# Up-projection of two FFNs by seven block products instead of eight

## The chip, the cores and the metric

The kernel runs on one core of a Trainium2 chip. Its engines work side by side, each on its own list of instructions in order: TensorE (PE), with its weight loads shown apart (PEld), VectorE (DVE), ScalarE (ACT), GpSimd (POOL), and SyncE (SP), which here issues all the DMAs. The metric is the time of one execution on the device in microseconds. Times before: 1180.17 us, the median of three runs (1176.22 to 1181.59).

## The reference

Two trunk layers over 512 latent tokens of 1024 channels, with 256 context tokens. Layer 0 has attention as its mixer, layer 1 a Fourier transform over channels and tokens; each layer ends in a gated FFN with a convolution of width 3 over the tokens. Around each sub-layer stand RMS norms and a modulation (shift, scale, gate) that is computed from a conditioning vector. What matters here is the FFN:

```
def conv_ffn(h, w_up, conv_w, conv_b, w_down):
    u = h @ w_up                                   # (512, 1024) @ (1024, 2 * 2816)
    up = jnp.pad(u, ((0, 0), (1, 1), (0, 0)))
    u = up[:, :-2] * conv_w[0] + up[:, 1:-1] * conv_w[1] + up[:, 2:] * conv_w[2] + conv_b
    gate, val = jnp.split(u, 2, axis=-1)
    return (jax.nn.silu(gate) * val) @ w_down      # (512, 2816) @ (2816, 1024)
...
x = x + g2 * rms_norm(conv_ffn(h, ffn_w_up[i], ...), norm_g[i, 3])
```

## The kernel before, in words

Channels lie on the 128 partitions, tokens along the free axis: `xT` is the stream, `yT` a sub-layer's result, each 8 channel tiles (`KC`) by 512 tokens in fp32. Every product is made of three: an operand is split into a high part (an ACT cast to fp32r, `h`) and a low part (DVE: source minus high part, `l`), and `mm3` (lines 89 to 92) issues high x high, high x low, low x high. `split` (L112, its two instructions on L113) does this for weights and activations. `hh` and `hl` hold the two parts of the FFN's input.

An FFN has 22 channel tiles `fi` of 128 hidden channels, each with a gate part and a value part. For one `fi`, `up_weights` (L943) loads 1 MB of weights (`raw`, three buffers, L120), splits the two halves (128 x 1024 each) into `wh` and `wl` (`wpair`, four buffers, L125), and `up_mm` (L979) makes 8 x 3 products of 512 columns for each half, into one PSUM bank (tag `mm`, six banks). `conv` (L984) turns the bank into a convolved tile `cv`: ACT does the middle tap and the bias (L994), DVE the other two taps (L995, L997), reading PSUM. `gated` (L1006) does the Silu on ACT (L1007), the product on DVE (L1008), and splits the result into a pair from `Pairs` (seven pairs of buffers of two tiles each), where it waits for the down-projection.

The first three `fi` (the six units in `first`, L1016 to L1083) are made while the input's second token half is still being worked out: in the first FFN they run beside the end of the attention's output boundary, in the second beside the end of the Fourier layer's, where the token factors and the shift are applied after the products (`fix`, L989 to L1001). `remod` and `mod_tiles` (L212, L282) make the modulated input: h = x * am * R + bm, then its two parts, odd channel tiles with POOL's help.

The rest goes by `HALVES`: 14 `fi`, then 8. After each part follows the down-projection over its `fi`, for 8 output tiles `d`: `weights(d)` loads and splits, `part(d, hs)` multiplies; the first part is copied to `yT` by ACT, the second added by DVE (L1102). In the second part the output tiles are first made for token half 0 (tile 0 for both), then `mid` starts what follows with that half, and the seven products for half 1 (L1134) are made beside it. In the first FFN, `gemv_jobs` (L368) computes the modulation of layer 1 meanwhile: 24 loads of 1 MB (`in_mod_r`), 48 operations of 1024 elements on DVE (L376, L379). It is a generator, and `pump` advances it: once after each `fi` and twice after each output tile `d` of the first part (`GP = [1, 2]`).

The order on each engine is that of a scheduler which takes the text's order and lets an instruction pass where an earlier one is not ready; `follow` and `fence` fix an order by hand. Buffers rotate in the order of allocation, so that a load for `raw` waits until the third buffer before it has been used up.

Of the kernel before, what the change touches and what calls it, by code (L numbers as in the profile page):

```python
# [10 lines left out]
F32 = mybir.dt.float32  # L11
F32R = mybir.dt.float32r
# [17 lines left out]
HALVES = [(0, 14), (14, 8)]  # L30
# [4 lines left out]
# what is traced where: how far work of one kind runs ahead of another kind's  # L35
# [32 lines left out]
def kernel(ctx: ExitStack, tc: tile.TileContext, a):  # L68
# [20 lines left out]
    def mm3(out, ah, al, bh, bl, start, stop):  # L89
        i = PE.matmul(out, lhsT=ah, rhs=bh, start=start, stop=False)  # L90
        PE.matmul(out, lhsT=ah, rhs=bl, start=False, stop=False)  # L91
        return i, PE.matmul(out, lhsT=al, rhs=bh, start=False, stop=stop)  # L92

    # issued after another one on the same engine
# [4 lines left out]
    # work that must not be issued ahead of the last instruction traced before a fence on its engine  # L99
# [61 lines left out]
    # products that keep the PE's clock up where it would have to wait  # L161
# [4 lines left out]
    # sums over channels: four column tiles of the PE hold a quarter of the tokens each  # L166
# [5 lines left out]
    # 1 / sqrt(sum / D + eps)  # L172
# [10 lines left out]
    # the same where only the time until the end counts: sums on all partitions at once  # L183
# [14 lines left out]
    # one quarter of the tokens per quadrant of partitions: side by side, then to all partitions  # L198
# [12 lines left out]
    # h = x * am * R + bm for several channel tiles, shared out over the engines  # L211
    def mod_tiles(items, R):  # L212
        for i, (h, l, src, am, bm) in enumerate(items):
            t = mk(cp, [P, HT], F32, "md_t", 4)
            if i % 2:
# [11 lines left out]
    # squares of y: summed over channel tiles by GpSimd, the last one by the PE  # L227
    class YStat:
# [8 lines left out]
        def add(self, pps, src, hs):  # L237
# [9 lines left out]
            # the halves of the last one share a tile where they come one after the other  # L247
# [26 lines left out]
    # x += gate * rms_norm(y) for one channel tile  # L274
# [7 lines left out]
    def remod(h, am, bm, R, ks=range(KC)):  # L282
        hs = halves[h]
        mod_tiles([(hh[:, k, hs], hl[:, k, hs], xT[:, k, hs], am[:, k:k + 1], bm[:, k:k + 1]) for k in ks], R)

    # x += gate * rms_norm(y); then the next sub-layer's modulated input
# [56 lines left out]
        # the factors: tokens on partitions, or on all partitions  # L343
# [23 lines left out]
    # adaLN off the critical path: products and sums on DVE, the sum over partitions on the PE  # L367
# [30 lines left out]
    # the same on the PE: four column tiles take a quarter of the columns each  # L398
# [27 lines left out]
    # output projection's weights for two channel tiles  # L426
# [10 lines left out]
    with ExitStack() as es:  # L437
# [998 lines left out]
```

## Time and profile before

| what | value |
|---|---|
| median of three runs | 1180.17 us |
| span of the profiled execution | 1176.5 us |
| its own time | the span is from the first instruction to the last; the median of the runs lies 3.7 us above it |
| PE busy | 1134.0 us, 6878 products, as many weight loads |
| DVE busy | 751.6 us, 1215 instructions |
| ACT busy | 512.2 us, 887 instructions |
| POOL busy | 201.1 us, 213 instructions |
| moved by DMA | 145.18 MB, mean 123 GB/s |

The page of the profile gives the busy time of each engine, and the span in 40 slices; further down the chain of work that ended last, and the groups of instructions that cost most, by line, engine and operation. A group's row reads: line, engine, operation, output <- inputs, shapes, count | busy us, mean ns of one | idle time of the engine just before, and what ended it. A row of a timeline reads: start in us, duration in us, engine, line, operation, output <- inputs, shape, count, and in brackets how long the engine sat idle before and what released it. Durations on DVE, ACT and PE hold an end that overlaps the next instruction, so that neighbours' starts lie closer together than the durations say. A row of the windows gives for a stretch of the span its length and the busy time of each engine in it, then the TensorE clock granted (1.00 is full speed), the busy share of the DMA engines and GB/s. `mm<-hh,wh` is an up-projection, `mm<-xh,wh` a down-projection.

### The profile page before, as it was taken

How to read it: one execution, taken by the hardware profiler on the slowest of the kernel's cores; microseconds unless marked ns; L12 is line 12 of the kernel's file. 1: busy time of each engine (PE TensorE's matmuls, PEld its weight loads, DVE VectorE, ACT ScalarE, POOL GpSimd, SP SyncE). 2: the span in 40 equal slices, each digit the busy share in tenths (PEclk: the TensorE clock that was granted, in tenths of full speed). 3: DMA queues.
4: the chain of work that ended last, by engine and by line, in shares of the span. 5: the costliest groups of instructions: out<-in, count | busy, mean ns of one | idle time of the engine just before them, and what ended most of it. 6: DMA issues, size and time to landing. Idle time of an engine off the chain costs nothing.

```text
span 1176.5 us, 17135 instructions
## 1 busy us (share of the span) xinstructions
PE 1134.0 (96%) x6878; PEld 946.1 (80%) x6878; DVE 751.6 (64%) x1215; ACT 512.2 (44%) x887; POOL 201.1 (17%) x213
## 2 busy tenths in 40 slices
PE   7999999999999999999999998988999999999995
PEld 4689898679898877777878998877788888888895
DVE  4673777675779685756665568988966532255555
ACT  3332356566554434322444445646644332234342
POOL 1132534222320000000000153663000000000013
PEclk9999999999999999999999999998999999999998
DMA  9432110874115353666622301621233222332112
GB/s 371 187 127 72 37 36 7 298 306 152 65 43 209 108 208 110 237 238 225 233 90 56 116 11 35 210 81 60 72 108 103 73 84 99 108 108 72 54 55 72
DMA packets 27127, 145.18 MB, mean 123 GB/s; under 512 B 2724, under 2 KB 7460, under 8 KB 14120
## 3 DMA queue, kind: packets, MB, share of 16 engines
q1 hardware_dynamic: 27048, 144.09, 35.0%
q8 instruction: 54, 0.88, 0.3%
q14 instruction: 25, 0.20, 0.1%
HBM read 141.98 MB, written 2.10 MB: 122 GB/s over the span
## 4 chain that ended last, share of the span: by engine, by line
PE 84%; DVE 11%; DMA 1%; ACT 1%; issue 1%; POOL 1%; SPq 0%; DVEq 0%; ACTq 0%; POOLq 0%
PE mm L90 24%; PE mm L92 23%; PE mm L91 23%; DVE md_t L278 2%; PE PT L786 2%; PE gm L405 1%; DVE hl L333 1%; PE O L90 1%; DVE wl L113 1%; DVE xT L280 1%; PE S L90 1%; PE O L91 1%; PE O L92 1%; PE S L92 1%; DMA xT<-in_xT 1%
## 5 line engine op out<-in xcount | busy, mean ns | idle before, releaser
L113 DVE TENSOR_TENSOR wl<-raw,wh 128x1024 fp32r<-128x1024 f32 (+1 forms) x139 | 167.6, 1210 | 207.8 <-ACT wh L113 207.5
L90 PE MATMUL mm<-hh,wh 128*128 128x512 f32 (+2 forms) x728 | 276.1, 379 | 0.0
L92 PE MATMUL mm<-hh,wl 128*128 128x512 f32 (+2 forms) x728 | 275.7, 379 | 0.0
L91 PE MATMUL mm<-hl,wh 128*128 128x512 f32 (+2 forms) x728 | 275.4, 378 | 0.0
L113 ACT CAST wh<-raw 128x1024 fp32r<-128x1024 f32 (+2 forms) x151 | 149.6, 999 | 183.4 <-PE mm L91 141.9
L90 PEld LDWEIGHTS mm<-hh,wh 128*128 128x128 f32 x728 | 137.7, 189 | 29.3 <-issue 1.2
L92 PEld LDWEIGHTS mm<-hh,wl 128*128 128x128 f32 x728 | 137.7, 189 | 27.9
L91 PEld LDWEIGHTS mm<-hl,wh 128*128 128x128 f32 x728 | 137.8, 189 | 27.5
L253 POOL TENSOR_TENSOR gacc<-gacc,sq 128x256 f32<-128x256 f32 (+1 forms) x35 | 31.5, 900 | 681.3 <-ACT sq L251 680.5
L90 PE MATMUL mm<-xh,wh 128*128 128x512 f32 (+1 forms) x368 | 131.5, 357 | 0.0
L91 PE MATMUL mm<-xl,wh 128*128 128x512 f32 (+1 forms) x368 | 130.6, 355 | 0.0
L92 PE MATMUL mm<-xh,wl 128*128 128x512 f32 (+1 forms) x368 | 130.5, 355 | 0.0
L90 PEld LDWEIGHTS mm<-xh,wh 128*128 128x128 f32 x368 | 69.2, 188 | 12.4 <-issue 1.2
L91 PEld LDWEIGHTS mm<-xl,wh 128*128 128x128 f32 x368 | 69.1, 188 | 11.1
L92 PEld LDWEIGHTS mm<-xh,wl 128*128 128x128 f32 x368 | 69.0, 187 | 11.0
L113 ACT CAST xh<-cv 128x512 fp32r<-128x512 f32 x44 | 27.3, 620 | 100.9 <-DVE cv L1008 100.9
L995 DVE SCALAR_TENSOR_TENSOR cv<-mm,cols,cv 128x511 f32<-128x511 f32 x83 | 61.8, 745 | 11.4 <-ACT cv L994 11.4
L994 ACT ACTIVATE cv<-mm,cols 128x512 f32<-128x512 f32 x83 | 64.2, 774 | 10.4 <-PE mm L92 10.4
L997 DVE SCALAR_TENSOR_TENSOR cv<-mm,cols,cv 128x511 f32<-128x511 f32 x83 | 62.2, 749 | 2.2
L1007 ACT ACTIVATE cv<-cv 128x512 f32<-128x512 f32 x44 | 27.8, 631 | 71.2 <-DVE cv L997 68.7
L379 DVE SCALAR_TENSOR_TENSOR gacc<-raw,scol,gacc 128x1024 f32<-128x1024 f32 x42 | 53.8, 1281 | 4.5 <-DMA raw<-in_mod_r 4.1
L91 PE MATMUL mm<-hl,xh 128*128 128x256 f32 (+1 forms) x160 | 47.3, 296 | 3.6 <-DVE hl L333 2.8
(358 smaller groups left out, 2238.7 us busy)
## 6 DMA issues: line engine op xcount, KB each, us to landing
raw<-in_w_up SPq DMA_DIRECT2D x44, 1024.0 KB, 5.0
raw<-in_mod_r SPq DMA_DIRECT2D x24, 1024.0 KB, 5.0
raw<-in_mod_p SPq DMA_DIRECT2D x16, 1024.0 KB, 6.4
raw<-in_w_down SPq DMA_DIRECT2D x16, 896.0 KB, 4.6
raw<-in_w_down SPq DMA_DIRECT2D x16, 512.0 KB, 3.7
raw<-in_w_in SPq DMA_DIRECT2D x6, 1024.0 KB, 5.0
raw<-in_w_out SPq DMA_DIRECT2D x4, 1024.0 KB, 6.0
raw<-in_w_f SPq DMA_DIRECT2D x8, 512.0 KB, 4.4
```

Of the source, the lines that this page charges most:

```text
L90: i = PE.matmul(out, lhsT=ah, rhs=bh, start=start, stop=False)
L91: PE.matmul(out, lhsT=ah, rhs=bl, start=False, stop=False)
L92: return i, PE.matmul(out, lhsT=al, rhs=bh, start=False, stop=stop)
L113: i = S.copy(out=h, in_=src), eng.tensor_tensor(out=l, in0=src, in1=f(h), op=ALU.subtract)
L253: G.tensor_tensor(out=self.acc[:, sl], in0=self.acc[:, sl], in1=sq[:, sl], op=ALU.add)
L278: m = V.scalar_tensor_tensor(out=t, in0=yT[:, k, hs], scalar=der[:, l, gi, k:k + 1], in1=R, op0=ALU.mult, op1=ALU.mult)
L379: held(V.scalar_tensor_tensor(out=acc, in0=w[:, i, :], scalar=scol[:, 0, k:k + 1], in1=acc, op0=ALU.mult, op1=ALU.add))
L786: PE.transpose(out=pt[:, j * P:(j + 1) * P], in_=Ps[j][:, off:off + P], identity=ident)
L994: S.activation(out=cv, in_=ps, func=AF.Identity, bias=bc, scale=wc[1])
L995: V.scalar_tensor_tensor(out=cv[:, 1:], in0=ps[:, :T - 1], scalar=wc[0], in1=cv[:, 1:], op0=ALU.mult, op1=ALU.add)
L997: V.scalar_tensor_tensor(out=cv[:, :T - 1], in0=ps[:, 1:], scalar=wc[2], in1=cv[:, :T - 1], op0=ALU.mult, op1=ALU.add)
L1007: S.activation(out=cg, in_=cg, func=AF.Silu)
```

## The change

For the 19 `fi` behind the first three, in both FFNs, the up-projection is made in blocks. The input is cut in two over channels (4 tiles each) and in two over tokens (256 each), the weights in two over channels and into gate and value: a 2 x 2 by 2 x 2 product, done by Strassen's scheme (in Winograd's form) with seven block products. Each is 4 x 3 products of 256 columns.

- `seven_inputs`, once for each FFN, forms four combinations of the input's blocks on DVE. It needs the unsplit input, so `remod` now leaves it in `yT` (`kept` in `mod_tiles`; even channel tiles get one more ACT instruction). It splits the four into three pairs of `spare` buffers and, for the fourth, over the place of `hh` and `hl` for channels 0 to 3 of token half 1.
- `seven_weights`, for each `fi`, forms four combinations of the weights' blocks on POOL (128 x 512 each) in a second `raw` buffer, and splits seven blocks instead of four: 3 of 128 x 512, 2 of 128 x 1024, in four `wpair` buffers.
- `seven_products` makes the products in two PSUM banks. Where banks hold sums, ACT copies a partial result out before another product is added on top; POOL adds two of them, DVE makes three sums. The result is `u` in SBUF (one buffer), and `conv` now reads it there instead of in PSUM.
- `HALVES` (14, 8) becomes `GROUPS` (8, 8, 6): three down-projections, the second and the third added to `yT`. `Pairs` shrinks from seven pairs to four, and three `spare` ones. All groups begin their first two output tiles without the last `fi`, which before was so in the last part only.
- `gemv_jobs` is no longer pumped after each `fi`, but twice after each output tile `d` of groups one and two (`GP = 2`).

```diff
-HALVES = [(0, 14), (14, 8)]
+GROUPS = [(0, 8), (8, 8), (16, 6)]
+FIRST = 3
-GP = [1, 2]
+GP = 2
...
+            if kept is not None and i % 2 == 0:
+                V.scalar_tensor_tensor(out=t, in0=src, scalar=am, in1=R, op0=ALU.mult, op1=ALU.mult)
+                S.activation(out=t, in_=t, func=AF.Identity, bias=bm, scale=1.0)
+                S.copy(out=h, in_=t)
+                V.tensor_tensor(out=l, in0=t, in1=f(h), op=ALU.subtract)
...
+    def seven_inputs(xp):
+        (b11, b12), (b21, b22) = blocks_of(yT)
+        hi, lo = blocks_of(hh), blocks_of(hl)
+        V.tensor_tensor(out=b11, in0=b12, in1=b11, op=ALU.subtract)
+        V.tensor_tensor(out=b12, in0=b22, in1=b12, op=ALU.subtract)
+        V.tensor_tensor(out=b22, in0=b22, in1=b11, op=ALU.subtract)
+        V.tensor_tensor(out=b21, in0=b21, in1=b22, op=ALU.subtract)
+        t3, t2, t4 = (xp.spare([P, KH, HT]) for _ in range(3))
+        t1 = hi[0][1], lo[0][1]
+        for (h, l), src in ((t3, b12), (t1, b11), (t2, b22), (t4, b21)):
+            split(h, l, src)
...
+    def seven_weights(l, fi):
+        r = raw([P, 2, KC, P], a["w_up"][l, fi])
+        s = mk(wp, [P, 4, KH, P], F32, "raw", 3)
+        (a11, a12), (a21, a22) = [[r[:, i, c * KH:(c + 1) * KH, :] for c in range(2)] for i in range(2)]
+        G.tensor_tensor(out=s[:, 2], in0=a11, in1=a21, op=ALU.subtract)
+        G.tensor_tensor(out=s[:, 0], in0=a21, in1=a22, op=ALU.add)
+        G.tensor_tensor(out=s[:, 1], in0=s[:, 0], in1=a11, op=ALU.subtract)
+        G.tensor_tensor(out=s[:, 3], in0=a12, in1=s[:, 1], op=ALU.subtract)
+        w = {}
+        for names, srcs in (("17", (a11, s[:, 2])), ("56", (s[:, 0:2],)), ("24", (r[:, :, KH:, :],)), ("3", (s[:, 3],))):
+            wh, wl = wpair([P, len(names), KH, P])
...
+    def seven_products(l, fi, pool, pps, bs):
...
+        one = product("1", 0, 0, True, True)
+        p1 = mk(cp, [P, HT], F32, "md_t", 4)
+        S.copy(out=p1, in_=ps[0][:, :HT])
+        seven = product("7", 1, 1, True, True)
+        follow(product("5", 1, 0, False, True)[0], seven[-1])
+        p57 = mk(cp, [P, T], F32, "sq", 2)
+        S.copy(out=p57, in_=ps[1])
+        follow(product("6", 0, 1, False, True)[0], one[-1])
+        product("2", 0, 0, False, True)
+        q = mk(cp, [P, HT], F32, "md_t", 4)
+        G.tensor_tensor(out=q, in0=p57[:, :HT], in1=p57[:, HT:], op=ALU.add)
+        S.copy(out=u[:, :HT], in_=ps[0][:, :HT])
+        V.tensor_tensor(out=p1, in0=ps[0][:, HT:], in1=p1, op=ALU.add)
+        V.tensor_tensor(out=u[:, 3 * HT:], in0=p1, in1=q, op=ALU.add)
+        product("4", 1, 1, False, True)
+        product("3", 1, 0, False, True)
+        V.tensor_tensor(out=u[:, HT:3 * HT].rearrange("p (a b) -> p a b", a=2),
+                        in0=ps[1].rearrange("p (a b) -> p a b", a=2),
+                        in1=p1.unsqueeze(1).to_broadcast([P, 2, HT]), op=ALU.add)
+        return u[:, :T], u[:, T:]
...
-            cv = mk(xp.pool, [P, T], F32, "cv%d" % i, 2)
+            cv = mk(xp.pool, [P, T], F32, "cv%d" % i, 2 - i)
...
+        bs = seven_inputs(xp)
+        for gi, (f0, nch) in enumerate(GROUPS):
+            end = gi == len(GROUPS) - 1
+            for fi in range(max(f0, FIRST), f0 + nch):
+                cc = [conv(fi, i, u) for i, u in enumerate(seven_products(l, fi, xp.pool, pps, bs))]
                 gated(fi, cc[0], cc[1], f0)
-                if gem is not None:
-                    pump(gem, GP[0])
...
-                if gem is not None and hf == 0:
-                    pump(gem, GP[1])
+                if gem is not None and not end:
+                    pump(gem, GP)
```

More of the change, by code (lines that the diff above doesn't have):

```diff
@@ new lines, in seven_weights @@
+    def seven_weights(l, fi):
[9 more added lines that the diff above has]
+            wh, wl = wpair([P, len(names), KH, P])
+            if len(srcs) == len(names):
+                for i, src in enumerate(srcs):
+                    split(wh[:, i], wl[:, i], src)
+            else:
+                split(wh, wl, srcs[0])
+            for i, n in enumerate(names):
+                w[n] = wh[:, i], wl[:, i]
+        return w
@@ new lines, in seven_products, with product @@
+    def seven_products(l, fi, pool, pps, bs):
+        w = seven_weights(l, fi)
+        ps = [mk(pps, [P, T], F32, "mm", 6) for _ in range(2)]
+        u = mk(pool, [P, 2 * T], F32, "u")
+        def product(n, b, h, first=False, last=False):
+            (wh, wl), (bh, bl) = w[n], bs[n]
+            m = []
+            for k in range(KH):
+                m += mm3(ps[b][:, halves[h]], wh[:, k, :], wl[:, k, :], bh[:, k, :], bl[:, k, :], first and k == 0,
+                    last and k == KH - 1, True)
+            return m
+        one = product("1", 0, 0, True, True)
[18 more added lines that the diff above has]
+        return u[:, :T], u[:, T:]
@@ L1407, in _layout @@
     out = {}
-    for h, (f0, n) in enumerate(HALVES):
+    for h, (f0, n) in enumerate(GROUPS):
         out["w_down%d" % h] = wd[:, f0:f0 + n].transpose(0, 3, 2, 1, 4)
```

73 lines of the change are left out of this document (33 added, 40 removed).

## The prediction

> **What bounds the kernel now.** I read the page first: the busy shares, then the chain of work that ended last.
>
> ```profile
> span 1176.5 us, 17135 instructions
> PE 1134.0 (96%) x6878; PEld 946.1 (80%) x6878; DVE 751.6 (64%) x1215; ACT 512.2 (44%) x887; POOL 201.1 (17%) x213
> ...
> PE 84%; DVE 11%; DMA 1%; ACT 1%; issue 1%; POOL 1%; SPq 0%; DVEq 0%; ACTq 0%; POOLq 0%
> ```
>
> The execution is 1176.5 us from first to last instruction; the median of the runs, 1180.17 us, has 3.7 us more around it. My sum is made against the 1176.5 and then added to the median. PE is busy for 96% and holds 84% of the chain, DVE 11%: a PE kernel, so fewer columns through PE should pay where PE waits for nobody. The view of windows shows where that is (columns: length, then PE, weight loads, DVE, ACT, POOL, clock, share of the DMA engines, GB/s).
>
> ```profile
> core 0: us, PE busy (x) PEld busy (x) DVE busy (x) ACT busy (x) POOL busy (x), PEclk, DMA share, GB/s
> ...
> 470.00:550.00 80.00, 80.00 (x362) 62.68 (x361) 51.03 (x54) 21.79 (x30) 0.00 (x0) 1.00 0.66 236
> ...
> 830.00:960.00 130.00, 130.00 (x556) 104.47 (x556) 84.30 (x114) 58.34 (x77) 0.00 (x0) 1.00 0.28 93
> ```
>
> 830 to 960 is the up-projection of the second FFN: PE 130 of 130 us, DVE 65%, ACT 45%, POOL nothing. 470 to 550, the down-projection of the first, is just as full of PE. So 19 of 22 channel tiles of each FFN (all but the three `first` ones) pass where only PE counts, with DVE a third idle. The question is what the change asks of DVE and POOL there.
>
> **PE's part.** In order of time, 51 products of 256 columns start between these two rows, and two ACT casts lie one whole tile (48 products of 512 columns) apart.
>
> ```profile
> 345.07 0.28 PE L90 MATMUL mm<-hh,wh 128*128 128x256 f32 x1
> ...
> 351.07 0.28 PE L92 MATMUL mm<-hh,wl 128*128 128x256 f32 x1
> ```
>
> ```profile
> 396.20 1.05 ACT L113 CAST wh<-raw 128x1024 fp32r<-128x1024 f32 x1 [0.48 <-PE mm L91]
> ...
> 407.45 1.05 ACT L113 CAST wh<-raw 128x1024 fp32r<-128x1024 f32 x1 [0.48 <-PE mm L91]
> ```
>
> 6.00/50 = 0.120 us per 256 columns, each with a weight load of its own; 11.25/48 = 0.234 us per 512. A tile was 48 x 0.234 = 11.25 us and becomes 7 x 4 x 3 = 84 x 0.120 = 10.08 us. If PE stays the bound, 38 tiles x 1.17 = 44 us are won; no more is in the change.
>
> **DVE's part.** Starts of neighbours on DVE give what each really takes, without the overlapped end:
>
> ```profile
> 355.15 0.74 DVE L995 SCALAR_TENSOR_TENSOR cv<-mm,cols,cv 128x511 f32<-128x511 f32 x1
> 355.81 1.21 DVE L113 TENSOR_TENSOR wl<-raw,wh 128x1024 fp32r<-128x1024 f32 x1
> 356.94 0.74 DVE L997 SCALAR_TENSOR_TENSOR cv<-mm,cols,cv 128x511 f32<-128x511 f32 x1
> ...
> 358.26 0.68 DVE L1008 TENSOR_TENSOR cv<-cv,cv 128x512 f32<-128x512 f32 x1
> 358.86 0.74 DVE L997 SCALAR_TENSOR_TENSOR cv<-mm,cols,cv 128x511 f32<-128x511 f32 x1
> ```
>
> ```profile
> 826.09 0.41 DVE L993 TENSOR_TENSOR sq<-mm,Rs 128x256 f32<-128x256 f32 x1
> 826.42 0.42 DVE L219 TENSOR_TENSOR hl<-md_t,hh 128x256 fp32r<-128x256 f32 x1
> ```
>
> 0.66 us for a convolution tap, 1.13 for 1024 elements, 0.60 for 512, 0.33 for 256. Before, a tile needed 2 x 1.13 (low parts of the weights), 4 x 0.66, 2 x 0.60 (gating) = 6.1 us. After: low parts of seven half-blocks instead of four (3 x 0.60 + 2 x 1.13 = 4.1), three sums that put the products together (0.33 + 0.33 + 0.60 = 1.3), the same 2.6 and 1.2: 9.2 us. By itself that still fits under 10.08. ACT gets 1536 more elements to cast (1.05 us per 1024, row above: 1.6) and 1024 to copy out of PSUM (about 1.1) on 45% of 11.25 = 5.1: 7.8 us, which fits.
>
> **POOL's part, and the price.** POOL was idle here; now it makes four sums of 512 elements and one of 256 for each tile, all from SBUF. What POOL does to DVE is seen in the Fourier stage, DVE first, POOL below:
>
> ```profile
> 747.18 1.65 DVE L1253 TENSOR_TENSOR gacc<-raw 128x512 f32<-128x512 f32 x1
> ...
> 749.08 0.67 DVE L1253 TENSOR_TENSOR yT<-raw 128x512 f32<-128x512 f32 x1
> ...
> 751.48 1.98 DVE L113 TENSOR_TENSOR wl<-yT,wh 128x1024 fp32r<-128x1024 f32 x1
> ...
> 753.71 1.43 DVE L1253 TENSOR_TENSOR gacc<-raw 128x512 f32<-128x512 f32 x1
> ```
>
> ```profile
> 747.00 1.27 POOL L1252 TENSOR_TENSOR yT<-raw 128x512 f32<-128x512 f32 x1 [1.16 <-DVE wl L113]
> 750.57 1.80 POOL L253 TENSOR_TENSOR acc<-acc,sq 128x512 f32<-128x512 f32 x1 [2.30 <-ACT sq L251]
> 752.34 2.26 POOL L1252 TENSOR_TENSOR gacc<-raw 128x512 f32<-128x512 f32 x1
> 754.60 1.71 POOL L253 TENSOR_TENSOR acc<-acc,sq 128x512 f32<-128x512 f32 x1
> ```
>
> The same DVE subtraction takes 0.67 us alone and 1.65 beside a POOL sum: it ends 0.56 after POOL's end at 748.27. At 750.57 to 756.3 they take strict turns: POOL ends 752.37, DVE 753.46, POOL 754.60, DVE 755.14, POOL 756.31. So a 512-element POOL sum holds DVE up for 1.14 to 1.17 us, and DVE's 512 take 0.54. This holds for a convolution tap with both operands in SBUF too:
>
> ```profile
> 824.07 1.23 DVE L997 SCALAR_TENSOR_TENSOR cv<-sq,cols,cv 128x511 f32<-128x511 f32 x1
> ...
> 827.75 0.74 DVE L997 SCALAR_TENSOR_TENSOR cv<-sq,cols,cv 128x511 f32<-128x511 f32 x1
> ```
>
> ```profile
> 823.83 0.92 POOL L216 TENSOR_TENSOR md_t<-xT,Rs 128x256 f32<-128x256 f32 x1 [1.75 <-DVE hl L219]
> ```
>
> but not for a DVE operation with one operand in PSUM: here three take 1.06 us, undisturbed, beside POOL's row.
>
> ```profile
> 703.42 1.06 DVE L1102 TENSOR_TENSOR yT<-yT,mm 128x256 f32<-128x256 f32 x3
> ```
>
> ```profile
> 701.67 5.63 POOL L253 TENSOR_TENSOR gacc<-gacc,sq 128x256 f32<-128x256 f32 x6 [0.36 <-ACT sq L251]
> ```
>
> The Trainium skill (SBUF — State Buffer, Who interferes with whom) says that a VectorE instruction with two SBUF inputs and a GpSimd instruction that reads SBUF exclude each other for the whole instruction; this speaks against the change. By that rule, with the whole 1.27 us of POOL's row each time, a tile would take DVE 9.2 + 4 x 1.27 + 0.6 = 14.9 us; the turns above show a little less, as starts and ends overlap.
>
> Now the four taps read `u` in SBUF instead of PSUM, so that nearly all of DVE's tile excludes POOL: 3584 elements of weights, 2044 of taps, 1024 of gating, 256 of sums = 6908 elements. At 0.54 us per 512 that is 7.3 us; POOL's 2304 at 1.17 per 512 are 5.3. The two together can't be done in less than 12.5 us a tile: longer than the 11.25 of before, whatever the order. The upper end is DVE in order, each POOL sum delaying it: 9.2 + 4 x (1.17 - 0.06 that overlaps) + 0.5 = 14.1. I take 13.4, near the middle: the turns in the trace are strict, but DVE's two PSUM sums and its waits for ACT can lie beside POOL.
>
> **Group edges give back, group starts cost.** While PE does a group's down-projection, DVE has room in the second FFN. There lie the first tile's splits (all but one, 3.5), POOL's four sums for the first two tiles (9), and the last tile's last sum, taps and gating (4.4), less 1.4 for the last product: 15.5 us a group. Weights for more than that have no buffers (four pairs, three raw). The first group has only the last of these (3.0), and starts with work of its own: `seven_inputs` is eight DVE operations of 1024, 8 x 1.13 = 9.1, behind what DVE still owes when PE ends the first tiles:
>
> ```profile
> 827.12 0.28 PE L92 MATMUL mm<-hh,xl 128*128 128x256 f32 x1
> ```
>
> ```profile
> 843.97 0.69 DVE L113 TENSOR_TENSOR xl<-cv,xh 128x512 fp32r<-128x512 f32 x1
> ```
>
> ```profile
> L113 DVE TENSOR_TENSOR wl<-raw,wh 128x1024 fp32r<-128x1024 f32 x3 | 3.7, 1221 | 0.0
> ```
>
> ```profile
> 356.76 0.28 PE L92 MATMUL mm<-hh,xl 128*128 128x256 f32 x1
> ```
>
> ```profile
> 365.57 0.68 DVE L113 TENSOR_TENSOR xl<-cv,xh 128x512 fp32r<-128x512 f32 x1
> ```
>
> ```profile
> L379 DVE SCALAR_TENSOR_TENSOR gacc<-raw,scol,gacc 128x1024 f32<-128x1024 f32 x2 | 2.6, 1276 | 0.0
> ```
>
> In the second FFN PE is done with them at 827.4 and DVE comes to their last split at 843.97; of these 16.6 us, three splits of later weights (3 x 1.13, the group's row) and three later taps (3 x 0.66) take 5.4: 11.2 owed. In the first FFN it is 356.9 to 365.57, of which two modulation products (2 x 1.19) and one split take 3.5: 5.2 owed.
>
> Second FFN, groups of 5, 8, 6 tiles: 5 x 13.4 - 3 + 9.1 + 11.2 = 84.3 for 56.2; 8 x 13.4 - 15.5 = 91.7 for 90; 6 x 13.4 - 15.5 = 64.9 for 67.5. Sum +27.
>
> First FFN: 78.3 for 56.2 (+22). The modulation jobs (`gemv_jobs`) are pumped only beside the down-projections now, two to each of 16 channel tiles of 24 x 0.234 = 5.6 us.
>
> ```profile
> L379 DVE SCALAR_TENSOR_TENSOR gacc<-raw,scol,gacc 128x1024 f32<-128x1024 f32 x42 | 53.8, 1281 | 4.5 <-DMA raw<-in_mod_r 4.1
> ...
> raw<-in_mod_r SPq DMA_DIRECT2D x24, 1024.0 KB, 5.0
> ```
>
> 48 operations of at most 1.28 are 61 us in 90 of PE's, beside 16 splits (18) and 8 additions (5): DVE is full, so that groups two and three get back only 7.5 (tail, first POOL sums): +10 and +5. Their 24 MB and 8 MB of weights in 90 us are 373 GB/s; the window at 470 moved 236 at a share of 0.66, 358 at a full one: +3. By buffers it is more: 5.0 us to land and 2.5 to use, about 8 a turn, three buffers, 2.5 loads a tile: 6.7 us, +17. I take +10. Sum +47.
>
> Ahead of the Fourier stage, PE's cover for the chain over DVE and POOL gets shorter, since the last group has 6 tiles instead of 8: 7 x 2 x 3 x 0.120 = 5.0 us, and PE already waits there:
>
> ```profile
> 707.36 0.42 PE L170 MATMUL misc<-gacc,ones 128*32 128x64 f32 x8 [2.13 <-POOL gacc L253]
> ```
>
> so +5. Before the output I take nothing; with too little cover there too it would be another 5. The modulated input is now kept in `yT`, with one more ACT cast of this kind for every second channel tile:
>
> ```profile
> 808.81 0.39 ACT L218 CAST hh<-md_t 128x256 fp32r<-128x256 f32 x1
> ```
>
> 16 x 0.39 = 6.2, of which most lies beside PE: +2 (0 to 6). The added third pass over `yT` goes beside products: nothing; uncovered it would be 16 x 0.6 = 10.
>
> 27 + 47 + 5 + 2 = +81: 1257.5 us for the execution, 1261 for the median. With 12.5 a tile (never under PE's 10.08) and +3 for the loads it is +41, 1221; with 14.1 and +17, +115, 1295.
>
> **Rivals.** *Edges hide it (faster).* Place: the starts of all groups. If the 9.1 and what DVE owes there are done ahead, under the first tiles, every group gets 15.5 back and the turns cost only 12.5, a group of 8 takes 84.5, the others PE's 50.4 and 60.5: -18 an FFN, with +10 left elsewhere -27: 1153. It decides as soon as a tile's average, edges in it, falls below 11.25. For it: DVE idles 35% at 830, and PE's gain is sure. Against: DVE is behind at both starts, and modulation fills the first FFN's down-projections. *It cancels:* 12.5 a tile and half the start hidden, about 1180. *Strict turns and queues in order (slower still).* ACT's copies of partial products, its casts and its Silu wait for PE, buffers and DVE in turn; a copy late by over 2.9 us (two products) stops PE, and `u` has one buffer. At 14.9 a tile, 38 x 1.5 = 57 us more: 1318. By the Trainium skill's rule above (SBUF — State Buffer, Who interferes with whom) a tile takes the same 14.9. For this case: ACT's load rises to 7.8; against: two products of slack each time. *That it isn't seven products* would show as 96 half products a tile; the diff names seven blocks, so I give this nothing.
>
> **Numbers.** Forecast 0.63, edges 0.20, cancelling 0.07, queues 0.10. A measurement of this kernel tells 0.5% from nothing. Likeliest 1261, its own range 1221 to 1295; to hold 8 in 10 it goes down to 1160, most of the way to the edges' case, and up to 1310. Faster 0.20, same 0.05 (1174 to 1186), slower 0.75.
>
> **What would show it.** In the up-projection: POOL with five operations a tile, DVE's low parts at up to twice 1.13 us, DVE near 95% busy, PE waiting some 3 us a tile with DVE or ACT as releaser, tiles 13.4 us apart in mid-group. In the first FFN's down-projection: raw loads back to back. Wrong if mid-group tiles are 10 to 11 us apart, or PE's idle time lies elsewhere.

## The result, and the profile after

The changed kernel takes 1295.86 us (median of four runs, 1293.54 to 1296.98), the kernel before beside it 1180.88 us: a ratio of 1.0975, 95% interval 1.0942 to 1.1009. It is slower by 9.7%. The profiled execution has a span of 1291.8 us, 115.3 above the 1176.5 of before. Lines L... below are those of the changed kernel; `conv`'s two taps on DVE are now L1078 and L1080, the four weight sums on POOL L982 to L985.

Three lines of the page of the changed kernel: span, busy times, and the chain that ended last.

```profile
span 1291.8 us, 20771 instructions
...
PE 1143.1 (88%) x8162; PEld 1015.1 (79%) x8162; DVE 1027.8 (80%) x1475; ACT 625.1 (48%) x1139; POOL 486.6 (38%) x403
...
DVE 22%; PE 18%; POOL 12%; issue 3%; ACT 3%; DMA 2%; DVEq 0%; POOLq 0%; ACTq 0%; SPq 0%
```

PE had 84% of the chain and has 18%; DVE and POOL together now have 34%. DVE's busy time grew by 276 us for 260 more instructions, over a microsecond each, which is more than most of its instructions take: old ones must have become longer. The groups by line show the convolution's taps among them (columns: count | busy us, mean ns | idle before).

```profile
L1078 DVE SCALAR_TENSOR_TENSOR cv<-u,cols,cv 128x511 f32<-128x511 f32 x76 | 102.0, 1376 | 4.4 <-ACT cv L1077 4.4
L1080 DVE SCALAR_TENSOR_TENSOR cv<-u,cols,cv 128x511 f32<-128x511 f32 x76 | 91.8, 1246 | 0.0
```

A tap was 0.74 us. The next rows show one tile late in the second FFN: DVE from the last sum of the tile before, then POOL, then DVE again one tile later, when no weights are left to be summed.

```profile
1084.99 0.68 DVE L1029 TENSOR_TENSOR u<-mm,md_t 128x512 f32<-128x512 f32 x1
...
1098.69 0.69 DVE L1029 TENSOR_TENSOR u<-mm,md_t 128x512 f32<-128x512 f32 x1
1099.30 1.43 DVE L116 TENSOR_TENSOR wl<-raw,wh 128x512 fp32r<-128x512 f32 x1
1100.65 3.44 DVE L1078 SCALAR_TENSOR_TENSOR cv<-u,cols,cv 128x511 f32<-128x511 f32 x2
1104.02 2.91 DVE L1080 SCALAR_TENSOR_TENSOR cv<-u,cols,cv 128x511 f32<-128x511 f32 x2
```

```profile
1098.91 1.27 POOL L982 TENSOR_TENSOR raw<-raw 128x512 f32<-128x512 f32 x1 [6.23 <-DVE wl L116]
1100.14 1.72 POOL L983 TENSOR_TENSOR raw<-raw 128x512 f32<-128x512 f32 x1
1101.94 1.61 POOL L984 TENSOR_TENSOR raw<-raw,raw 128x512 f32<-128x512 f32 x1
1103.62 1.61 POOL L985 TENSOR_TENSOR raw<-raw,raw 128x512 f32<-128x512 f32 x1
```

```profile
1114.36 1.46 DVE L1078 SCALAR_TENSOR_TENSOR cv<-u,cols,cv 128x511 f32<-128x511 f32 x2 [0.35 <-ACT cv L1077]
1115.74 1.41 DVE L1080 SCALAR_TENSOR_TENSOR cv<-u,cols,cv 128x511 f32<-128x511 f32 x2
```

Four taps take 6.3 us beside POOL's sums and 2.8 us without them, and POOL's sums stretch too, from 1.27 to 1.6 and 1.7 us. The windows in the middle of a group show who is full (length, PE, weight loads, DVE, ACT, POOL, clock, DMA share, GB/s).

```profile
500.00:580.00 80.00, 66.78 (x482) 65.13 (x483) 79.37 (x83) 42.99 (x72) 43.04 (x30) 0.87 0.20 73
...
1072.00:1112.00 40.00, 33.96 (x246) 33.55 (x247) 39.34 (x41) 21.68 (x36) 21.46 (x15) 0.87 0.19 67
```

DVE is busy 99% of the time, stretched instructions included, where it was 65%. The last sum of a tile (L1029) comes every 13.7 us here (512.54, 526.23, 539.98, 553.66 us in the first FFN, 1084.99 and 1098.69 in the rows above); a tile of before took 11.25. But PE's own waits name another engine:

```profile
PE mm L93 <- ACT md_t L1014: 52.0, 26, 3.2
PE mm L95 <- DVE wl L116: 20.5, 23, 2.0
```

52 us of waits for an ACT copy: product 6 goes into the bank from which ACT still has to copy product 1, and that copy stands in ACT's queue behind the previous tile's middle taps (L1077), which wait for DVE. After most of these waits PE also runs at half its rate for a while, as here:

```profile
1101.30 0.39 PE L93 MATMUL mm<-zh,wh 128*128 128x256 f32 x1 [2.06 <-ACT md_t L1014]
...
1103.14 0.41 PE L93 MATMUL mm<-zh,wh 128*128 128x256 f32 x1
1103.36 0.41 PE L94 MATMUL mm<-zl,wh 128*128 128x256 f32 x1
...
1105.77 0.28 PE L93 MATMUL mm<-zh,wh 128*128 128x256 f32 x1
1105.89 0.28 PE L94 MATMUL mm<-zl,wh 128*128 128x256 f32 x1
```

Products start 0.21 to 0.22 us apart until 1105.06, about 3.7 us, then 0.12. Is this wait the cause, or a symptom? The trace alone doesn't say.

Where the 115 us lie, from the first product of each phase to the first of the next (us; read from PE's timeline, good to some 0.2 us; the phases of before with 14 and 8 channel tiles are added up for comparison, and the figures in brackets are the groups of 8, 8 and 6 channel tiles, called A, B and C below):

| stage | before | after | difference |
|---|---|---|---|
| first FFN, up (from 280) | 293.5 | 327.1 (145.6 + 104.9 + 76.6) | +33.6 |
| first FFN, down | 129.4 | 154.3 (59.0 + 57.4 + 37.9) | +24.9 |
| Fourier layer and norms | 72.2 | 81.8 | +9.6 |
| second FFN, up | 263.1 | 308.9 (131.6 + 103.3 + 74.0) | +45.8 |
| second FFN, down | 125.3 | 127.1 (44.9 + 44.8 + 37.4) | +1.8 |

### The profile page after: what moved, and what is told of

Read it like the earlier page. It is cut to its first block, busy times and chain, and to the rows that moved or that the text cites. A ratio compares the mean times of both kernels' runs of the same rounds, so it can differ in the third digit from the quotient of the medians.

```text
span 1291.8 us, 20771 instructions
## 1 busy us (share of the span) xinstructions
PE 1143.1 (88%) x8162; PEld 1015.1 (79%) x8162; DVE 1027.8 (80%) x1475; ACT 625.1 (48%) x1139; POOL 486.6 (38%) x403
## 4 chain that ended last, share of the span: by engine, by line
DVE 22%; PE 18%; POOL 12%; issue 3%; ACT 3%; DMA 2%; DVEq 0%; POOLq 0%; ACTq 0%; SPq 0%
DVE wl L116 7%; PE mm L95 6%; PE mm L94 6%; PE mm L93 6%; POOL raw L983 2%; POOL raw L984 2%; POOL raw L985 2%; POOL raw L982 2%; ACT wh L116 2%; POOL md_t L1023 2%; DVE md_t L286 2%; DVE xl L116 2%; DVE cv L1078 1%; DVE cv L1091 1%; DVE cv L1080 1%
## 5 line engine op out<-in xcount | busy, mean ns | idle before, releaser
L116 DVE TENSOR_TENSOR wl<-raw,wh 128x1024 fp32r<-128x1024 f32 (+3 forms) x253 | 280.2, 1119 | 67.7 <-ACT wh L116 67.1
L116 ACT CAST wh<-raw 128x512 fp32r<-128x512 f32 (+2 forms) x265 | 215.4, 838 | 159.8 <-PE mm L94 59.0
L95 PE MATMUL mm<-hh,wl 128*128 128x256 f32 (+1 forms) x728 | 211.5, 291 | 11.0 <-DVE wl L116 10.9
L93 PE MATMUL mm<-hh,wh 128*128 128x256 f32 (+1 forms) x728 | 211.7, 291 | 1.2 <-DVE sq L1076 1.2
L94 PE MATMUL mm<-hl,wh 128*128 128x256 f32 (+1 forms) x728 | 211.2, 290 | 0.0
L93 PE MATMUL mm<-zh,wh 128*128 128x256 f32 x456 | 141.5, 310 | 66.8 <-ACT md_t L1014 52.0
L982 POOL TENSOR_TENSOR raw<-raw 128x512 f32<-128x512 f32 x38 | 50.5, 1329 | 360.8 <-DVE wl L116 167.0
L94 PE MATMUL mm<-zl,wh 128*128 128x256 f32 x456 | 136.8, 300 | 4.1 <-DVE zl L116 4.1
L95 PE MATMUL mm<-zh,wl 128*128 128x256 f32 x456 | 136.8, 300 | 2.3 <-DVE wl L116 2.3
L1078 DVE SCALAR_TENSOR_TENSOR cv<-u,cols,cv 128x511 f32<-128x511 f32 x76 | 102.0, 1376 | 4.4 <-ACT cv L1077 4.4
L1077 ACT ACTIVATE cv<-u,cols 128x512 f32<-128x512 f32 x76 | 57.8, 807 | 87.9 <-DVE u L1029 87.9
L94 PEld LDWEIGHTS mm<-zl,wh 128*128 128x128 f32 x456 | 96.2, 211 | 4.4 <-DVE zl L116 4.4
L1080 DVE SCALAR_TENSOR_TENSOR cv<-u,cols,cv 128x511 f32<-128x511 f32 x76 | 91.8, 1246 | 0.0
L1023 POOL TENSOR_TENSOR md_t<-sq 128x256 f32<-128x256 f32 x38 | 54.6, 1438 | 89.8 <-ACT sq L1019 89.8
```

The costliest lines, as they stand in the source:

```text
L93: i = PE.matmul(out, lhsT=ah, rhs=bh, start=start, stop=False, skip_group_check=skip)
L94: PE.matmul(out, lhsT=ah, rhs=bl, start=False, stop=False, skip_group_check=skip)
L116: i = S.copy(out=h, in_=src), eng.tensor_tensor(out=l, in0=src, in1=f(h), op=ALU.subtract)
L982: G.tensor_tensor(out=s[:, 2], in0=a11, in1=a21, op=ALU.subtract)
L1023: G.tensor_tensor(out=q, in0=p57[:, :HT], in1=p57[:, HT:], op=ALU.add)
L1077: S.activation(out=cv, in_=ps, func=AF.Identity, bias=bc, scale=wc[1])
```

## The experiments

Three theories of the up-projection. **L**: POOL's instructions and DVE's that have both operands in SBUF shut each other out, and this sets the tile. **Q**: ACT's queue and the wait of product 6 set it. **D**: DVE simply has too much work of its own. All kernels below are edits of the changed kernel, timed beside the kernel before; ratios are to the kernel before.

**POOL writes, but reads nothing.**

```diff
-        G.tensor_tensor(out=s[:, 2], in0=a11, in1=a21, op=ALU.subtract)
+        G.memset(s[:, 2], 0.5)
...
```

(and the three other sums alike.)

> Leaves out part of the computation: GpSimd's four weight sums of each tile are replaced by four fills with a constant of the same four buffers, so the products work on wrong blocks; every buffer, every split and every instruction of the other engines stays. Theory L (GpSimd's sums, which read two tiles of SBUF, and VectorE's taps and splits, which do too, keep each other out, and this sets the tile): the taps come back to about 0.72 us each from 1.25 to 1.38, the tile in the middle of a group falls from 13.7 us to 10.1 to 10.8, near TensorE's own 84 x 0.120 = 10.08, the whole to 1160 to 1210 us. Rival Q (ScalarE's queue: product 6 waits for the copy of product 1, which stands behind the previous tile's middle taps, which wait for VectorE's last sum): that order is as before, the wait on the copy stays near 2 us a tile, the tile stays at 13 or above, the whole above 1260. Rival D (the amount of VectorE's own work fills the tile, whoever else runs): the tile stays at 13 or above, VectorE 95% busy.

Measured 1180.0 us, ratio 1.0014 (0.9983 to 1.0044). The taps are back (minimum, median and maximum in ns), and the window in mid-group:

```profile
L1078 DVE SCALAR_TENSOR_TENSOR cv<-u,cols,cv x76: 736/751/754, 371.0 to 1128.2; 128x511 f32<-128x511 f32 x76
```

```profile
480.00:540.00 60.00, 59.67 (x506) 59.20 (x506) 56.33 (x84) 43.37 (x72) 32.49 (x26) 1.00 0.27 99
```

```profile
487.55 0.69 DVE L1029 TENSOR_TENSOR u<-mm,md_t 128x512 f32<-128x512 f32 x1
...
497.62 0.69 DVE L1029 TENSOR_TENSOR u<-mm,md_t 128x512 f32<-128x512 f32 x1
```

The tile is 10.07 us (the last sum at 487.55, 497.62, 507.69): PE's own 10.08, with PE full and DVE at 94%. The wait on L1014's copy falls from 52.0 us to 3.2 in all, with ACT's queue untouched: it was a symptom. D falls as well: DVE's own instructions, 56.33/60 x 10.07 = 9.4 us a tile, fit. L holds. The Trainium skill (SBUF — State Buffer, Who interferes with whom) says that VectorE with two SBUF inputs contends with a GpSimd instruction that reads SBUF, not with one that only writes it; the fills, at 0.53 us each and beside taps of 0.75, agree.

**POOL reads one tile instead of two.**

```diff
-        G.tensor_tensor(out=s[:, 2], in0=a11, in1=a21, op=ALU.subtract)
-        G.tensor_tensor(out=s[:, 0], in0=a21, in1=a22, op=ALU.add)
+        G.tensor_copy(out=s[:, 2], in_=a11)
+        G.tensor_copy(out=s[:, 0], in_=a21)
...
```

> Leaves out part of the computation: GpSimd's four weight sums of each tile become four copies of one block, so that GpSimd reads one tile of SBUF in each and not two. Theory L in the form that any GpSimd instruction that reads SBUF keeps VectorE's two-input instructions out: the taps stay at 1.1 us or more, the tile at 12.5 to 13.7 us (less only by what a copy is shorter than a sum), the whole at 1240 to 1295. In the form that only two-input instructions on both sides keep each other out: taps at 0.75 us, the tile at 10.0 to 10.5, the whole at 1175 to 1200, as with the fills.

Measured 1205.74 us, ratio 1.0221 (1.0187 to 1.0256), a tile every 11.02 us: neither range. The first tap's median of 0.75 us (L1078) looks like the second form, the second tap's of 1.09 (L1080) like the first; the timeline (POOL, then DVE) shows the turns:

```profile
504.70 0.61 POOL L982 COPY raw<-raw 128x512 f32<-128x512 f32 x1 [6.16 <-DVE wl L116]
505.25 1.08 POOL L983 COPY raw<-raw 128x512 f32<-128x512 f32 x1
506.39 1.01 POOL L984 COPY raw<-raw 128x512 f32<-128x512 f32 x1
507.47 0.95 POOL L985 COPY raw<-raw 128x512 f32<-128x512 f32 x1
```

```profile
506.18 1.76 DVE L1078 SCALAR_TENSOR_TENSOR cv<-u,cols,cv 128x511 f32<-128x511 f32 x2 [0.33 <-ACT cv L1077]
507.87 2.24 DVE L1080 SCALAR_TENSOR_TENSOR cv<-u,cols,cv 128x511 f32<-128x511 f32 x2
```

The first copy, beside a DVE sum with an operand in PSUM, takes 0.61 us; the next three are stretched to about 1 us, and the four taps take 3.9 us instead of 2.8. One-input reads are shut out as well; they are only short: 9.4 + 4 x 0.61 = 11.8 is the most that full turns would give, 11.02 came. I had put the price of a copy too near to that of a sum. One tap's median alone would have misled here.

**Only two of the four sums.**

```diff
-        G.tensor_tensor(out=s[:, 0], in0=a21, in1=a22, op=ALU.add)
-        G.tensor_tensor(out=s[:, 1], in0=s[:, 0], in1=a11, op=ALU.subtract)
+        G.memset(s[:, 0], 0.5)
+        G.memset(s[:, 1], 0.5)
```

> Leaves out part of the computation: the second and third of GpSimd's four sums become fills, the first and the last stay sums. Theory L, in proportion: each sum costs the tile about 0.92 us ((13.7 less 10.0) / 4), so two cost half: 11.6 to 12.1 us a tile, the whole at 1230 to 1245. If VectorE has room under TensorE's 10.08 us, so that the first sums are free and the last ones dear: 10.1 to 11.0 a tile, the whole at 1185 to 1215.

Measured 1227.35 us, ratio 1.0401 (1.0363 to 1.0439), a tile every 11.70 us: the tile is where the proportion puts it, the whole 3 us under the range, nearer to it than to the other theory's. Two sums bring DVE to 99%:

```profile
490.00:556.00 66.00, 58.59 (x492) 57.56 (x491) 65.37 (x81) 40.29 (x67) 23.06 (x27) 1.00 0.24 87
```

9.4 + 2 x 1.27 = 11.9, against 11.70: each sum adds nearly its whole length to DVE's tile.

**The taps read PSUM.**

```diff
-        return u[:, :T], u[:, T:]
+        return (u[:, :T], ps[0]), (u[:, T:], ps[1])
...
-            S.activation(out=cv, in_=ps, func=AF.Identity, bias=bc, scale=wc[1])
+            if type(ps) is tuple:
+                m, ps = ps
+            else:
+                m = ps
+            S.activation(out=cv, in_=m, func=AF.Identity, bias=bc, scale=wc[1])
```

> Leaves out part of the computation: the side taps of the convolution read the two PSUM banks of the products instead of the combined sums in SBUF (the middle tap still reads the sums), so each tap has one input in SBUF and one in PSUM, as the taps of the kernel before had. Theory L (an instruction of VectorE with two inputs in SBUF and a GpSimd instruction that reads SBUF shut each other out): the taps come back to 0.75 us with GpSimd's sums as they are; VectorE loses then only what the sums take beyond the four taps' 3.0 us, about 2.1 of 5.1 us a tile, so the tile goes from 13.7 to 11.3 to 12.3 us, the whole to 1225 to 1255. If GpSimd slows VectorE whatever its operands, or the later release of the banks stops TensorE: taps at 1.2 us or more or the tile at 13 or above, the whole at 1280 or above.

Measured 1241.99 us, ratio 1.0519 (1.0485 to 1.0554), a tile every 11.77 us, as L had it. DVE, then POOL (DVE's lines are four higher in this kernel):

```profile
508.29 1.39 DVE L1082 SCALAR_TENSOR_TENSOR cv<-mm,cols,cv 128x511 f32<-128x511 f32 x2
509.61 1.39 DVE L1084 SCALAR_TENSOR_TENSOR cv<-mm,cols,cv 128x511 f32<-128x511 f32 x2
510.92 0.67 DVE L116 TENSOR_TENSOR wl<-raw,wh 128x512 fp32r<-128x512 f32 x1
511.52 1.77 DVE L1095 TENSOR_TENSOR cv<-cv,cv 128x512 f32<-128x512 f32 x1
513.22 2.36 DVE L116 TENSOR_TENSOR wl<-raw,wh 128x512 fp32r<-128x512 f32 x2
```

```profile
509.58 1.30 POOL L984 TENSOR_TENSOR raw<-raw,raw 128x512 f32<-128x512 f32 x1
510.96 1.78 POOL L985 TENSOR_TENSOR raw<-raw,raw 128x512 f32<-128x512 f32 x1
512.71 1.19 POOL L1023 TENSOR_TENSOR md_t<-sq 128x256 f32<-128x256 f32 x1
```

With one operand in PSUM four taps take 2.6 us beside POOL's sums, undisturbed, and POOL's L984 too keeps its 1.30; the price then falls on the gating product (1.77 for 0.68) and on the splits behind it. So the operand's place decides, and 1.9 of the 3.6 us a tile came from moving the taps' source from PSUM to SBUF.

**The sums on DVE.** `V.tensor_tensor` for `G.tensor_tensor` in L982 to L985.

> The four weight sums of each tile go from GpSimd to VectorE; nothing is left out. Theory L: VectorE gets four instructions of about 0.6 us more, but loses the time in which GpSimd keeps it out (some 4.5 us a tile), so the tile falls from 13.7 to about 12.1 us and the whole to 1215 to 1250, taken at 1232. Rival Q: VectorE's last sum comes no earlier, the whole stays at 1280 to 1300. Rival D: VectorE is full with its own work and gets 2.4 us more a tile: about 16 us a tile, the whole at 1360 to 1390.

Measured 1250.02 us, ratio 1.0590 (1.0549 to 1.0632) where the changed kernel has 1.0975, at the upper end of the range for L. A tile takes 11.3 us on average ((570.52 - 491.69)/7 between last sums), less than the 12.1 that L had: the tile is better than expected, and the rest costs more. DVE with four more instructions of 0.6 us is faster than DVE beside POOL. It is full:

```profile
500.00:565.00 65.00, 56.75 (x459) 54.31 (x459) 65.00 (x100) 41.77 (x67) 16.30 (x5) 1.00 0.21 74
```

So this version of the change is bound by DVE at about the 11.25 us that PE needed before: nothing is won in mid-group, and the costs elsewhere stay.

**The sums shared.** The first two on POOL, the last two on DVE.

```diff
-        G.tensor_tensor(out=s[:, 1], in0=s[:, 0], in1=a11, op=ALU.subtract)
-        G.tensor_tensor(out=s[:, 3], in0=a12, in1=s[:, 1], op=ALU.subtract)
+        V.tensor_tensor(out=s[:, 1], in0=s[:, 0], in1=a11, op=ALU.subtract)
+        V.tensor_tensor(out=s[:, 3], in0=a12, in1=s[:, 1], op=ALU.subtract)
```

> The first two of the four weight sums stay on GpSimd, the last two go to VectorE; nothing is left out. Theory L: the two sums on GpSimd lengthen the tile to about 11.2 us (as with two fills), and there VectorE is busy for 99% of the time, so its two sums of 0.6 us come on top: 12.2 to 12.6 us a tile, the whole at 1260 to 1280, between all on GpSimd (1296) and all on VectorE (1250). If work shared between the two runs side by side: below VectorE alone, 11.0 us a tile or less, the whole at 1225 to 1240.

Measured 1286.1 us, ratio 1.0908 (1.0875 to 1.0942); a tile takes 12.6 us ((579.77 - 504.12)/6), the upper end for L, and the whole is 6 us above its range. Sharing doesn't run side by side. The expectation's 11.2 us for two sums on POOL was too low: they had taken 11.70, and with that the same addition gives 12.9. It also left out a wait: DVE now stands in its own queue until POOL's second sum is there, 25 times and 50.0 us in all, and in the rows that sum is late because it and a DVE split take turns. How much of this wait the whole pays was not told apart.

```profile
504.72 1.45 DVE L116 TENSOR_TENSOR wl<-raw,wh 128x512 fp32r<-128x512 f32 x1
507.34 0.69 DVE L984 TENSOR_TENSOR raw<-raw,raw 128x512 f32<-128x512 f32 x1 [1.17 <-POOL raw L983]
```

**A bank of their own for products 1 and 2.**

```diff
-        one = product("1", 0, 0, True, True)
+        ps.append(mk(pps, [P, T], F32, "misc", 2))
+        one = product("1", 2, 0, True, True)
...
-        follow(product("6", 0, 1, False, True)[0], one[-1])
-        product("2", 0, 0, False, True)
+        product("6", 0, 1, True, True)
+        product("2", 2, 0, False, True)
```

(and the copies of product 1 and of `u`'s first block read `ps[2]`.)

> Products 1 and 2 go to a PSUM bank of their own, so that product 6 no longer waits until ScalarE has copied product 1; nothing is left out. Rival Q: the wait of 2.0 us a tile on that copy and the slow products behind it go, the tile falls to about 12.3 us, the whole to 1235 to 1255. Theory L: VectorE stays 99% busy in the middle of a group and sets the tile; the wait only moves, to product 2 or to the splits; the tile stays at 13.4 to 13.8, the whole at 1280 to 1300.

Measured 1289.89 us, ratio 1.0931 (1.0887 to 1.0974); the interval overlaps that of the changed kernel. The window in mid-group and PE's first waits:

```profile
500.00:580.00 80.00, 65.38 (x515) 61.61 (x514) 79.38 (x81) 42.43 (x70) 44.73 (x31) 1.00 0.21 73
```

```profile
PE misc L95 <- DVE wl L116: 33.6, 25, 1.8
PE mm L95 <- DVE wl L116: 21.7, 33, 3.1
PE misc L93 <- ACT md_t L1015: 17.8, 24, 0.8
```

The big wait is cut up, the granted clock is back from 0.87 to 1.00, and DVE is as full as before: a tile still takes 13.5 us (530.35, 543.89, 557.42). Q falls; the slow products cost little, because PE only arrived earlier at the next wait for DVE.

**The first FFN's down-projections.** Two parts taken away one by one: the 24 loads of the modulation's weights, and 42 of its 48 sums on DVE.

```diff
-                w = raw([P, 2, D], a["mod_r"][v, kk])
+                w = xT[:, :4, :].rearrange("p (i a) b -> p i (a b)", i=2)
```

> Leaves out part of the computation: in the down-projections of the first FFN the sums for the second layer's modulation are taken over tiles of x that are on chip, so that their 24 loads of 1 MB are not made (their VectorE instructions stay). If the loads (the ring of three raw buffers and the rate of the DMA queues) set those phases: the two phases fall from 59 and 57 us to 45 to 47 each, as in the second FFN, the whole to about 1270. If VectorE's work for these sums sets them: both stay at 55 or above, the whole at 1285 to 1300.

```diff
-                        held(V.scalar_tensor_tensor(out=acc, in0=w[:, i, :], scalar=scol[:, 0, k:k + 1], in1=acc,
+                        held(V.scalar_tensor_tensor(out=acc[:, :n], in0=w[:, i, :n], scalar=scol[:, 0, k:k + 1], in1=acc[:, :n],
```

(with `n = D if k == 0 else 8`.)

> Leaves out part of the computation: of VectorE's 48 sums for the second layer's modulation, 42 work on 8 of 1024 columns; all 24 loads of 1 MB stay, and everything else. If VectorE's time for these sums (1.28 us each, now all in the first FFN's two down-projections of 5.6 us a channel tile) sets those phases: they fall from 59 and 57 us to 45 to 48 each, the whole to 1265 to 1275. If the loads do (the ring of raw buffers and the queues' rate): taking the loads away moved the two phases only to 54.6 and 51.5, so with the loads left in they stay at 54 or above, the whole at 1285 or above.

Without the loads 1288.36 us (ratio 1.0931, 1.0884 to 1.0978), with short sums 1284.13 (1.0888, 1.0858 to 1.0918). Both expectations were wrong in their either-or: the phases fall from 59.0 and 57.4 us to 54.6 and 51.5 without loads, to 51.7 and 51.2 with short sums, not to the second FFN's 45. The wholes say little here: both lie within 1% of the changed kernel's 1295.86. The windows of these phases, of the changed kernel, without the loads, and with short sums:

```profile
426.00:484.60 58.60, 51.37 (x220) 36.43 (x219) 45.47 (x45) 15.23 (x22) 3.70 (x3) 0.97 0.81 296
589.60:646.90 57.30, 51.79 (x224) 37.38 (x223) 47.42 (x51) 12.64 (x17) 5.91 (x4) 0.97 0.72 267
```

```profile
424.00:478.50 54.50, 48.69 (x213) 37.31 (x211) 46.89 (x46) 16.77 (x24) 11.62 (x8) 0.97 0.25 87
```

```profile
427.00:478.80 51.80, 49.27 (x225) 36.65 (x224) 23.56 (x49) 15.27 (x22) 2.93 (x2) 1.00 0.89 340
```

Neither DVE (78%) nor the DMA engines (0.81) are full throughout. Without loads DVE still has 46.9 us to do; with short sums the DMA share is 0.89, and PE is kept busy some 4 us longer than the 45 of the second FFN, among other things by the modulation's own sums over partitions. Taking away either the loads or the sums saves 4 to 7 us of the 13 to 14 in each phase; what stays with both away was not tried.

**No `seven_inputs`.** The function's body becomes a list of blocks of `hh` and `hl`.

```diff
-        V.tensor_tensor(out=b11, in0=b12, in1=b11, op=ALU.subtract)
...
-        for (h, l), src in ((t3, b12), (t1, b11), (t2, b22), (t4, b21)):
-            split(h, l, src)
-        return {"1": (hi[0][0], lo[0][0]), "2": (hi[1][0], lo[1][0]), "3": (hi[1][1], lo[1][1]), "4": t4, "5": t1,
-                "6": t2, "7": t3}
+        return {n: (hi[c][h], lo[c][h]) for n, c, h in (("1", 0, 0), ("2", 1, 0), ("3", 1, 1), ("4", 1, 1), ("5", 0, 1),
+                                                        ("6", 1, 0), ("7", 0, 1))}
```

> Leaves out part of the computation: the four differences of the activations' blocks and their four splits, which stand between the last ordinary tile and the first seven-block tile of each FFN; the products take blocks of the input as it is. If that row of VectorE work is what the start of the seven-block tiles costs: the first FFN's group A falls from 145.6 us by 5 to 14, the second's from 131.6 by 15 to 20, the whole to 1262 to 1275. If it lies beside products that TensorE still has to make, or the tiles behind it, which VectorE paces, only take its place: under 8 us in all, the whole at 1285 or above.

Measured 1281.8 us, ratio 1.0871 (1.0842 to 1.0900). Group A of the first FFN falls by 3.7 us (145.6 to 141.9), that of the second by 11.1 (131.6 to 120.5); about 15 us in all, and between the two theories. In the first FFN most of it lies beside other work, in the second most of it counts.

**All three away** (fills, short sums, no `seven_inputs`).

> Leaves out all three at once: fills for GpSimd's four sums, the modulation's sums cut to 8 columns, no differences of the activations' blocks. If the account is whole, this is before's own time less what seven products for eight save on TensorE (38 tiles by 1.2 us, 45 us), plus the part of the Fourier stage that grew without the sums (about 5 us) and 1.6 us of smaller groups, less the 4 us by which the modulation's sums lengthened before's own down-projections: 1130 to 1142 us. If one of the three only covers another loss: 1150 or above.

Measured 1156.11 us, ratio 0.9809 (0.9780 to 0.9838): 14 us above the range, and on the side of the other outcome, that another loss was covered. Stage by stage against before: up-projections -27.4 and -17.9 us, together about PE's 44 us; but the first FFN's down-projections stay at +11.9, the Fourier stage at +8.1, the second FFN's down-projections at +2.1. My account had counted the down-projections as free once the sums were short.

What the fills' run says in the same way: with POOL out of the way the up-projections come to -24.9 and -5.2 us, and the down-projections (+22.4 and +1.6) and the Fourier stage (+5.5) take all of it back. So in these runs the scheme with fills in place of its weight sums only equals the kernel before. No complete version that beats the kernel before was found; of the runs here only the one with all three away is faster, and it leaves out parts of the computation. Mixing ordinary and seven-block tiles, so that DVE's slack in the one pays for the other, wasn't tried.

## Why the prediction was right, and where its sizes were off

- **PE's part.** 84 x 0.120 = 10.08 us: with the fills a tile took 10.07. Right.
- **DVE's and POOL's part.** Bounds of 12.5 and 14.1 us, taken 13.4: 13.7 measured, with DVE at 99%. The reason, strict turns of DVE and POOL over SBUF, is what fills, copies, two sums and taps from PSUM each showed. DVE's own 9.2 was 9.4. The least of 12.5, and the choice of 13.4, allowed for DVE's two PSUM sums beside POOL's. In the tile shown above only one of them does lie there, L1029, for half a microsecond (1098.91 to 1099.38); the other, L1025, starts at 1096.70, while POOL is idle. The mechanism was right.
- **Group edges give back.** This is the term of the sum that was most off: 15.5 us a group in the second FFN. From 13.7 a tile, groups of 8 and 6 would take 109.6 and 82.2; they took 103.3 and 74.0, so 6.3 and 8.2 came back. The step that failed is "POOL's four sums for the first two tiles" during the down-projection. POOL's rows of the second FFN's second down-projection (1122.6 to 1167.4) show when they were made:

```profile
1144.55 1.29 POOL L982 TENSOR_TENSOR raw<-raw 128x512 f32<-128x512 f32 x1 [26.82 <-DMA raw<-in_w_up]
...
1164.16 1.29 POOL L982 TENSOR_TENSOR raw<-raw 128x512 f32<-128x512 f32 x1 [13.48 <-DVE wl L116]
```

  The first tile's sums begin when their load has come, the second's only 3 us before PE goes back to the up-projection, when a split of DVE's has freed a `raw` buffer: each tile now takes two of the three. That is 17 us of the miss in the second FFN (15.5 + 15.5 against 14.5). In the first FFN, 4.7 and 5.6 came back for the 7.5 predicted.
- **Group starts cost.** Forecast: 9.1 for `seven_inputs` and 11.2 owed in the second FFN. Measured: 11.1 for `seven_inputs` (12.6 with POOL out of the way, 117.5 against 104.9). What was owed is about 5, an estimate: with all three away group A is still 104.9 where 105.6 of before less 5 x 1.17 would give 99.7. In the first FFN 3.7 instead of 9.1, and the rest lay beside other work. Group A of the second FFN came to +26.0 (131.6 for 105.6) against the +28 of the sum. That of the first came to +11.8 against +22: before reaches its ninth channel tile at 413.8, 133.8 us from the same start, where the changed kernel needs 145.6.
- **Loads and modulation in the first FFN's down-projections.** Taken at +10 within bounds that reached +17; +24.9 measured, 22.4 even with the fills. Failed step: I let DVE's 61 us and the loads' turns compete for one bound each, and priced only what exceeded PE. They alternate. In the first of the two phases the DMA queue waits for DVE to be done with a buffer, most of all here (us in total, times, longest):

```profile
SPq L125 <- DVE gacc L388: 30.9, 12, 5.2
```

  DVE waits 6.1 us there for these loads, PE 7.2 us for splits and sums, and PE is busy for 51.4 us where the second FFN's phase has 44.8. Neither DVE nor the DMA engines are full, and taking away either the loads or the sums gives only a third to a half.
- **Ahead of the Fourier stage.** +5 forecast, +9.6 measured, 5.5 to 8.1 in the runs without POOL's reads. The sign was right; no run changes the shorter cover alone, what the rest is was not tested, and the +2 for the modulated input can't be told from it.
- **Before the output** nothing was taken, and nothing came (13.1 us from the last product to the end, before and after).
- **Rivals.** "Strict turns and queues in order" named ACT's late copies as what stops PE, and the trace has just these waits, 52 us of them, with a half-rate PE behind them. But with the copy out of the way the tile stayed at 13.5: a visible wait of the busiest-looking engine, yet not the bound. Its price of 14.9 a tile was not reached. "Edges hide it" failed at its own condition: `raw` buffers let too little be done ahead.

In sum the forecast was 34 us too low: 17 from the edges of the second FFN, 15 from the first FFN's down-projections, 3 from the Fourier stage (9.6 for 5 and 2), and smaller terms of both signs; the first FFN's group A, taken 10 us too high, hid part of the miss. The 1295.86 us lie at the upper end of the sum's own range of 1221 to 1295. That end had been reached with 14.1 us a tile and +17 for the loads; it came instead from 13.7 a tile, edges that gave back half and +24.9 in the down-projections.

## What to carry to other kernels

Work given to an idle GpSimd isn't free for VectorE. Where VectorE's instructions have two operands in SBUF and GpSimd's read SBUF, add GpSimd's whole time to VectorE's, as the most that the turns can cost, and compare the sum with the tile. Here that gave 14.5 us for the 13.7 measured with four sums (9.4 + 4 x 1.27), 11.9 for 11.70 with two, and 11.8 for 11.02 with four copies. The same sums on VectorE itself took only 0.6 us each. Before a result is moved from PSUM to SBUF, look who reads it next: here the taps, undisturbed with one operand in PSUM, had to take turns with GpSimd once both were in SBUF. And when a wait shows up on the bounding engine, find out which engine is full in that window before mending the wait.

## What the runs showed of the hardware that was not expected

- After a wait of 2.06 us PE started products 0.21 us apart instead of 0.12 for about 3.7 us (the rows above), in the middle of a group (after one of 2.13 us at 501.42 they stayed at 0.12); the granted clock of such windows was 0.87, and 1.00 with products 1 and 2 in a bank of their own, where the waits were at most 0.8 us on the same copy and 1.5 us on a split.
- A GpSimd copy of 128 x 512 takes 0.61 us alone, a fill 0.53, a sum 1.27; copies were stretched to about 1 us beside VectorE's two-input instructions, the fills' median was 0.53 everywhere.
